# Issuing a decoder layer's input-row DMA transposes from SyncE instead of ScalarE, with its filler and priority tables refitted

## The chip, the cores and the metric

The kernel runs on one core of a Trainium2 chip. The metric is the device time of one execution in microseconds. Three runs of the kernel before gave 1943.07, 1945.29 and 1947.21 us (median 1945.29). A separate execution under the hardware profiler took 1942.91 us, of which 1941.2 us lie between its first and its last instruction (the span).

## The reference

One layer of a decoder over 2048 rows of 1024 float32 numbers:

```python
h = rms_norm(x, attn_norm_g)
z = h @ w_in                                   # 1024 x 2304
q, k, v, gate_b, gate_c, xc = split(z)         # q: 8 heads of 64; k, v: 2 heads of 64; gates and xc: 512 each
q, k = rms_norm(q, q_norm_g), rms_norm(k, k_norm_g)
y_attn = sliding_window_attention(q, k, v, sinks)        # window 128, blocks of 128 rows
y_conv = gate_b * conv3(gate_c * xc, conv_w)             # causal, over rows
y = concat(rms_norm(y_attn, attn_out_g), rms_norm(y_conv, conv_out_g))
x = x + y @ w_out
x = x + square(relu(rms_norm(x, mlp_norm_g) @ w_up)) @ w_down     # 1024 x 4096 and back
```

## The kernel before, in words

**Numbers.** Products are made of float32 numbers split into a high and a low part (`fp32r` tiles in pairs): the high part is a copy on ScalarE, the low part a subtraction on VectorE, and each product is three matmuls (`mm3`, lines 272 to 276: high by high, high by low, low by high).

**Stages.** The rows go through the mixers (attention and convolution) in four chunks of 512 rows (`mixers`, called for c = 0 to 3, each chunk four tiles of 128 rows, t = 0 to 3). This part takes the first 640 us or so. The MLP follows over all rows, in a seven-product scheme for 2 x 2 blocks (`u` in line 1485, `d` in line 1602), and takes the rest.

**Work inside a chunk.** A chunk has a chain of small steps for the attention of each block of 128 rows (`qk_norm`, `qk_transpose`, `softmax`, `values`) and a supply of long matmul groups that depend on little: the convolution's products pc, px and pb (`conv_pair`), the output projection's convolution half (`out_projection(c, 1, ..)`, tiles `pout`), and the projection of the next chunk's q, k and v (`project_qkv`, tiles `pz`). The generator `besides` hands these groups out in small pieces, and `fill(n)` puts n such pieces between two steps of the attention chain. How many go where is the table `FILL` (line 88): per chunk a pair, then four numbers groups of five, one per block. `PRIO` (line 86) holds priority offsets per chunk for fourteen kinds of steps (`ahead(i)`). A scheduler turns the program with these priorities into one in-order queue for each engine and for each engine's DMA issues; an engine does not pass a waiting instruction.

**The next chunk's rows.** While chunk c is computed, `prepare` (lines 380 to 447) makes the transposed and split input rows `h_a` of chunk c + 1, in four steps for each tile t:

- `fetch(t)` loads the tile's rows (`xt_a`, line 388; SyncE's queue).
- `halves(t)` takes the row norms (line 283 on ScalarE; GpSimd's lines 180 and 181 make the reciprocal root), scales (line 290, VectorE), takes the float32 numbers apart into their two 16-bit planes with two copies on ScalarE (line 403, `half_a`), and issues a DMA transpose of the planes back over `xt_a`: one transfer of 512 KB for t < 2 (line 407), two of 256 KB for t = 2 and 3 (line 410). That is 6 transposes a chunk and 18 in all (chunks 1 to 3 are prepared this way).
- `whole(t)` puts the planes together again with four copies on VectorE (line 417), which wait for the transposes.
- `split(t)` makes the high and low parts `h_a` (line 424 on ScalarE, line 425 on VectorE).

`EARLIER` (line 70) says after which pieces of the second convolution pair the first five steps of `prepare` are handed out; the rest are handed out three pieces apart in the output projection. For t < 2 the planes lie in buffers that the residual rows `x` of the chunk use afterwards (line 1027), so the load of those rows for t = 2 and 3 can start only when `split(0)` and `split(1)` are done.

**The convolution's norm factor.** `PC` (line 69) says after which piece of the output projection the sums for that factor are made (`pc`, line 1040); VectorE (line 1050 or 1053) and GpSimd (lines 180, 181 and, in chunk 0, 1055) turn them into `rc`, which VectorE's line 991 needs to add a `pout` result to the residual rows `x`. Line 991 also frees the PSUM bank: there are three for the `pout`, `pz` and convolution groups.

**Queues of transfers.** SyncE's queue issues, in program order as scheduled, nearly all loads and stores: stores of split weights (line 218) in chunk 0, raw weight loads (line 226: `raw_wc`, `raw_wx`, `raw_wb`, `raw_wo`), reloads of split weights in later chunks (line 235), the rows. ScalarE's and GpSimd's queues issue a few others. Each of SyncE's and ScalarE's transfers takes one of eight completion semaphores in turn, and waits until the transfer that had it has landed.

Of the kernel before, what the change touches and what calls it, by code (L numbers as in the profile page):

```python
# [11 lines left out]
U16 = mybir.dt.uint16  # L12
# [53 lines left out]
EARLY = 4  # L66
DOWN_BUFS = {"u": 2, "x1": 7}
UP_BUFS = {"w": 17, "u2": 3, "f11": 2, "u4": 2, "f12": 2, "s1": 1, "s2": 1, "s4": 1, "st": 5}
PC = (2, 1)
EARLIER = (16, 18, 23, 35, 38)  # L70

CHP = CH + 32
STEPS = 3
# [9 lines left out]

PRIO = ((60, 0, 160, -130, 30, 0, 20, -10, 0, 0, 0, 300, 0, 10), (160, -60, -120, -60, 40, 0, 20, 40, 0, -150, 0, 0, 0, -120), (80, 0, 10, 0, 40, 0, 200, -40, 0, -60, 320, 120, 0, 0), (230, 20, 180, 240, 0, 0, 40, 40, 0, 0, 0, 30, 0, 0), (160, 80, 0, 10, 0, 0, 20, -20, -20, 0, 0, 120, 0, 0))

FILL = (((14, 15), (9, 9, 11, 8, 1), (9, 6, 8, 8, 2), (10, 11, 5, 8, 4), (11, 10, 9, 6, 0)), ((25, 15), (9, 16, 11, 8, 1), (9, 10, 11, 3, 2), (13, 12, 15, 6, 5), (9, 13, 11, 5, 2)), ((20, 17), (9, 16, 11, 10, 1), (9, 5, 11, 7, 2), (16, 7, 15, 2, 6), (9, 15, 10, 5, 1)), ((27, 6), (9, 9, 5, 6, 3), (7, 7, 7, 9, 5), (4, 11, 9, 7, 8), (11, 3, 9, 3, 3)))

# [1 line left out]
def hymba_layer(  # L93
# [19 lines left out]
    nc = tc.nc  # L113
# [33 lines left out]
    def row(tag, name, bufs, dt=F32):  # L147

        return pool.tile([P, D], dt, tag=tag, name=name, bufs=bufs)
# [35 lines left out]
    def ahead(i):  # L185

        offset = PRIO[stage[0]][i]
        return tc.high_priority(offset=offset) if offset else nullcontext()
# [77 lines left out]
    @contextmanager  # L266
    def behind():

        with tc.issue_after(gates["act"]), tc.issue_after(gates["dve"]):
            yield  # L270
# [7 lines left out]
    def norm_stats(xt, name, rs=None, junk=None):  # L278
        if junk is None:
            junk = pool.tile([P, CHP], F32, tag="s2", name=f"junk_{name}", bufs=4)  # L280
        junk = junk.bitcast(BF16)[:, :D]
        ss = small.tile([P, 1], F32, tag="ss", name=f"ss_{name}", bufs=2)
        nc.scalar.activation(junk, xt, AF.Square, scale=D**-0.5, accum_out=ss)
        if rs is None:
            rs = small.tile([P, 1], F32, tag="rs", name=f"rs_{name}", bufs=2)
        rsqrt(rs, ss)
        return rs

    def scaled(xt, rs, gb):
        nc.vector.scalar_tensor_tensor(xt, xt, rs, gb, op0=ALU.mult, op1=ALU.mult)  # L290
# [88 lines left out]
    def parts(pool_, tag, name):  # L379
        return [pool_.tile([P, KD, CH], F32R, tag=f"{tag}{s}", name=f"{tag}{s}_{name}", bufs=1) for s in range(2)]  # L380

    def prepare(src, r0, gb, dst, name):

        xs, places, turned_ = {}, {}, {}

        def fetch(t):
            xs[t] = row("xt", f"xt_{name}_{t}", 2)
            nc.sync.dma_start(xs[t], src[r0 + t * P : r0 + (t + 1) * P, :])

        def halves(t):  # L390
            if t < 2:
                place = row("x1", f"half_{name}_{t}", NT)
                places[t] = [place[:, i * BW : (i + 1) * BW] for i in range(2)]
            else:
                places[t] = [
                    pool.tile([P, CHP], F32, tag="s2", name=f"half_{name}_{t}_{i}", bufs=4)[:, :BW] for i in range(2)
                ]
            xt = xs[t]
            with ahead(8), behind():
                scaled(xt, norm_stats(xt, f"{name}_{t}", junk=places[t][0]), gb)  # L400
                pairs = xt.bitcast(U16).rearrange("p (c i) -> p i c", i=2)
                for i, plane in enumerate(places[t]):
                    nc.scalar.copy(plane.bitcast(U16), pairs[:, i])
                turned_[t] = xt.bitcast(U16).rearrange("p (i k t) -> p i k t", i=2, k=KD)
                if t < 2:
                    out = xt.bitcast(U16).rearrange("p (k t) -> p k t", t=P)
                    nc.scalar.dma_start_transpose(out, place.bitcast(U16))
                else:
                    for i, plane in enumerate(places[t]):
                        nc.scalar.dma_start_transpose(turned_[t][:, i], plane.bitcast(U16))  # L410

        def whole(t):
            with ahead(9), behind():
                for n, raw in enumerate(places[t]):
                    pairs = raw.bitcast(U16).rearrange("p (k t i) -> p i k t", k=KH, i=2)
                    for i in range(2):
                        nc.vector.tensor_copy(pairs[:, i], turned_[t][:, i, n * KH : (n + 1) * KH])

        def split(t):
            with ahead(9), behind():  # L420
                for n, raw in enumerate(places[t]):
                    raw = raw.rearrange("p (k t) -> p k t", k=KH)
                    dh, dl = (d[:, n * KH : (n + 1) * KH, t * P : (t + 1) * P] for d in dst)
                    nc.scalar.copy(dh, raw)
                    nc.vector.tensor_tensor(dl, raw, dh.bitcast(F32), op=ALU.subtract)

        fetch(0)
        fetch(1)
        yield
        for t in range(2):  # L430
            halves(t)
            yield
        for t in range(2):
            whole(t)
            fetch(t + 2)
            yield
        dst += parts(pool, "h", name)
        for t in range(NT):
            split(t)
            if t < 2:  # L440
                halves(t + 2)
            if 0 < t < NT - 1:
                whole(t + 1)
            yield
# [218 lines left out]
    with tc.tile_pool(name="mix_small", bufs=1) as mix_small, tc.tile_pool(name="mix", bufs=1) as mix:  # L663
# [342 lines left out]
        def besides(c, before, h, yt, rc, x1, h_next, z_next):  # L1006
# [6 lines left out]
            else:  # L1013
                steps = range(PC[0] + 1)
            for j in range(2):
                for n, _ in enumerate(conv_pair(c, h, j, yt, ssc)):
                    if blocks and n % X_EVERY == 0:
                        next(blocks, None)
                    if j and not blocks and n in EARLIER:
                        next(steps)  # L1020
# [9 lines left out]
            for i, _ in enumerate(steps):  # L1030
                if c + 1 == NCHUNK:
                    yield
                for j in range(STEPS):
                    next(out, None)
                    yield
                    if (i, j) == PC:
                        factors.update((c, 1, t) for t in range(NT))
# [24 lines left out]
        def mixers(c, before, h, z):  # L1062


            last = c + 1 == NCHUNK
            n_fill = FILL[c]
            stage[0] = c
# [574 lines left out]
```

## Time and profile before

| | us |
|---|---|
| median of three runs | 1945.29 |
| profiled execution | 1942.91 |
| its span | 1941.2 |
| TensorE busy in the span | 1911.1 |
| VectorE, ScalarE, GpSimd busy | 1221.1, 850.4, 281.7 |
| DMA transposes: issues | 18, from ScalarE's queue |

A row of the timeline gives the start, the duration, the engine, the line of the kernel, the operation, output and inputs, how many such instructions are merged, and in brackets how long the engine was idle before the first of them and what ended that. ACTq and SPq are the issuing of DMAs by ScalarE and SyncE, which the busy times leave out. In a row of the windows each engine has its busy time and its number of instructions, and behind them stand the granted TensorE clock as a share of full speed, the mean busy share of the 16 DMA engines and the bytes moved per second. A matmul's recorded duration is longer than its spacing from the next one, since matmuls overlap; a 512-column one starts 0.23 us after the one before when nothing holds it.

### The profile page before, as it was taken

The page shows a single profiled execution, that of the slowest core. Times are in us where ns is not written, and L with a number is a line of the kernel's source. Part 1 is how long each engine was busy: PE and PEld are TensorE (multiplying, and loading weights), DVE is VectorE, ACT ScalarE, POOL GpSimd, SP SyncE. Part 2 cuts the span into 40 slices and gives each one's busy share as a digit, 9 for nine tenths or more (in the row PEclk, how much of TensorE's full clock was granted, in tenths as well). Part 3 has the DMA queues.
Part 4 walks back from the last instruction along what each step waited for, and adds up shares of the span by engine and source line. Part 5 has one row for each costly group of instructions (what it writes and reads, how often), then busy time and mean ns, then how long its engine had stood idle before and what let it go on. Part 6 is the DMA issues. An engine that isn't in the chain of part 4 may idle for free.

```text
span 1941.2 us, 24490 instructions
## 1 busy us (share of the span) xinstructions
PE 1911.1 (98%) x8834; PEld 1588.8 (82%) x8834; DVE 1221.1 (63%) x1905; ACT 850.4 (44%) x1581; POOL 281.7 (15%) x477
## 2 busy tenths in 40 slices
PE   9979999999899999999999999999999999999999
PEld 8868887888788888888888888888888888888887
DVE  4876567546648759998878766666544334447441
ACT  6554455435535337445565555554422332232220
POOL 2121312302131111222201111111000000100000
PEclk9989999999999999999999999999999999999999
DMA  9996858356567868878676544437964447766641
GB/s 299 317 255 198 275 221 267 133 217 225 176 230 264 292 210 271 249 210 241 202 231 225 184 147 152 159 124 295 375 224 138 148 161 237 260 228 207 204 152 55
DMA packets 257946, 420.11 MB, mean 216 GB/s; under 512 B 76824, under 2 KB 161568, under 8 KB 245024
## 3 DMA queue, kind: packets, MB, share of 16 engines
q1 hardware_dynamic: 203840, 336.59, 51.8%
q0 software_dynamic: 15424, 51.40, 6.9%
q10 hardware_dynamic: 38560, 30.55, 5.3%
q8 instruction: 70, 1.15, 0.2%
q14 instruction: 52, 0.43, 0.1%
HBM read 286.35 MB, written 125.83 MB: 212 GB/s over the span
## 4 chain that ended last, share of the span: by engine, by line
PE 80%; DVE 1%; ACT 1%; POOL 1%; ACTq 1%; issue 0%; DMA 0%; DVEq 0%
PE u L1485 31%; PE d L1602 31%; PE pout L274 2%; PE pout L275 2%; PE pout L276 2%; PE pz L274 1%; PE pz L276 1%; PE pz L275 1%; PE px_c L274 1%; PE px_c L276 1%; PE px_c L275 1%; PE pb_c L274 1%; PE pb_c L276 1%; PE po_b L838 1%; PE pb_c L275 1%; PE pc_c L275 1%
## 5 line engine op out<-in xcount | busy, mean ns | idle before, releaser
L1485 PE MATMUL u<-op_x,wop 128*128 128x512 f32 x2688 | 609.8, 389 | 0.0
L1602 PE MATMUL d<-op_w,op_f 128*128 128x512 f32 x2691 | 609.5, 389 | 0.0
L1485 PEld LDWEIGHTS u<-op_x,wop 128*128 128x128 f32 x2688 | 504.5, 188 | 105.1 <-issue 0.6
L1602 PEld LDWEIGHTS d<-op_w,op_f 128*128 128x128 f32 x2691 | 504.8, 188 | 104.7
L460 DVE TENSOR_TENSOR op_f<-op_f 128x1024 fp32r<-128x1024 f32 x112 | 136.8, 1224 | 235.8 <-ACT op_f L459 235.3
L459 ACT CAST op_f<-op_f 128x1024 fp32r<-128x1024 f32 x112 | 117.5, 1051 | 352.2 <-DMA op_f<-fop 342.2
L478 ACT CAST wop<-wu 128x512 fp32r<-128x512 f32 x156 | 96.2, 619 | 90.6 <-PE u L1485 88.2
L479 DVE TENSOR_TENSOR wop<-wu,wop 128x512 fp32r<-128x512 f32 x156 | 110.8, 712 | 32.3 <-DMA wu<-in_w_up_dram 20.1
L1221 POOL DMA_DIRECT2D fop<-s x96 | 52.1, 542 | 441.1 <-DVE s L1224 434.5
L1227 DVE TENSOR_TENSOR u<-u,u 128x512 f32<-128x512 f32 x128 | 87.7, 685 | 21.2 <-PE u L1485 20.9
L460 DVE TENSOR_TENSOR op_w<-raw,op_w 128x1024 fp32r<-128x1024 f32 x56 | 68.3, 1221 | 27.0 <-ACT op_w L459 26.8
L459 ACT CAST op_w<-raw 128x1024 fp32r<-128x1024 f32 x56 | 58.8, 1052 | 46.3 <-PE d L1602 24.2
L1233 ACT ACTIVATE u<-u 128x512 f32<-128x512 f32 x64 | 40.5, 632 | 58.9 <-DVE u L1227 56.8
L799 POOL TENSOR_SCALAR_AFFINE_SELECT pp_b<-pp_b 128x512 fp32r<-128x512 f32 x60 | 42.5, 720 | 149.3 <-ACT pp_b L792 115.3
L767 ACT ACTIVATE sc_b<-sc_b,ngm_b 128x128 f32<-128x128 f32 x128 | 49.7, 390 | 28.3 <-DVE ngm_b L764 26.4
L274 PE MATMUL pout<-w_wo,yt_c 128*128 128x512 f32 x128 | 53.2, 418 | 8.4 <-DVE x L991 8.0
L750 PE MATMUL psc_b<-kw,qt_b 128*128 128x256 f32 (+1 forms) x256 | 51.6, 292 | 6.0 <-DVE qt_b L729 5.1
L1434 POOL DMA_DIRECT2D wds<-raw x16 | 8.5, 533 | 330.5 <-DVE raw L1432 330.5
L275 PE MATMUL pout<-w_wo,yt_c 128*128 128x512 f32 x128 | 52.3, 409 | 1.6 <-DVE w_wo L247 1.6
L479 DVE TENSOR_TENSOR wop<-wu_s,wop 128x512 fp32r<-128x512 f32 x64 | 45.9, 718 | 12.3 <-ACT wop L478 12.2
L761 DVE COPY_PREDICATED sc_b<-later,psc_b 128x128 f32<-128x128 int32 x120 | 29.0, 295 | 38.8 <-ACT sc_b L758 38.6
L478 ACT CAST wop<-wu_s 128x512 fp32r<-128x512 f32 x64 | 39.4, 620 | 30.1 <-PE u L1485 24.5
(241 smaller groups left out, 3159.2 us busy)
## 6 DMA issues: line engine op xcount, KB each, us to landing
op_f<-fop SPq DMA_DIRECT2D x112, 512.0 KB, 4.3
raw<-in_w_down_dram SPq DMA_DIRECT2D x72, 512.0 KB, 4.4
wu<-in_w_up_dram SPq DMA_DIRECT2D x128, 256.0 KB, 3.7
w_wo<-wo SPq DMA_DIRECT2D x24, 1024.0 KB, 6.8
fop<-s POOLq DMA_DIRECT2D x96, 256.0 KB, 2.8
fop<-u ACTq DMA_DIRECT2D x64, 256.0 KB, 2.6
op_x<-xop SPq DMA_DIRECT2D x28, 512.0 KB, 6.0
w_q<-q SPq DMA_DIRECT2D x12, 1024.0 KB, 6.9
```

Source lines behind the costliest of these rows:

```text
L274: nc.tensor.matmul(ps, st(0), mv(0), start=first, stop=False)
L275: nc.tensor.matmul(ps, st(0), mv(1), start=False, stop=False)
L276: last_sum[0] = nc.tensor.matmul(ps, st(1), mv(0), start=False, stop=last).ins
L459: nc.scalar.copy(op[:, 0], raw)
L460: nc.vector.tensor_tensor(op[:, 1], raw, op[:, 0].bitcast(F32), op=ALU.subtract)
L478: splits.append(nc.scalar.copy(hi, blk).ins)
L479: lows.append(nc.vector.tensor_tensor(lo, blk, hi.bitcast(F32), op=ALU.subtract).ins)
L750: nc.tensor.matmul(ps[:, j].rearrange("p s k -> p (s k)")[:, :nk], qt[:, pr, j, :], kw[:, r, kv, :, :].rearrange("p s k -> p (s k)")[:, :n ...
L1221: eng.dma_start(fop_dram[tb][ORDER_DOWN.index(i)][n // 2][:, n % 2], b)
L1227: return nc.vector.tensor_tensor(dst, ps, b, op=ALU.add).ins
L1485: nc.tensor.matmul(pt, wops[i][:, a, k, :], xops[tb, p][k // 2][:, b, k % 2, :], start=p not in GOES_ON and k + j == 0, stop=k + j == NB + ...
L1602: nc.tensor.matmul(ps[tb][j][:, cs], fs[tb][:, a, k, j * P : (j + 1) * P], w[:, b, k, cs], start=first and p not in GOES_ON and k + n == 0 ...
```

## The change

The DMA transposes of `prepare` are issued by SyncE. They take their place in SyncE's queue among the loads and stores. `PC` and `EARLIER` have other numbers, and so have the tables `FILL` and `PRIO`, of which one line each is shown in part; 13 of the 88 numbers of `FILL` and 14 of the 70 of `PRIO` differ. No operation is added or removed: the instructions are the same, in another order on each engine.

```diff
-PC = (2, 1)
-EARLIER = (16, 18, 23, 35, 38)
+PC = (1, 2)
+EARLIER = (14, 19, 23, 35, 37)
...
-FILL = (((14, 15), (9, 9, 11, 8, 1), (9, 6, 8, 8, 2), (10, 11, 5, 8, 4), (11, 10, 9, 6, 0)),
+FILL = (((18, 15), (9, 9, 11, 8, 1), (9, 6, 4, 8, 2), (10, 11, 5, 8, 4), (11, 10, 9, 2, 0)),
...
                 if t < 2:
                     out = xt.bitcast(U16).rearrange("p (k t) -> p k t", t=P)
-                    nc.scalar.dma_start_transpose(out, place.bitcast(U16))
+                    nc.sync.dma_start_transpose(out, place.bitcast(U16))
                 else:
                     for i, plane in enumerate(places[t]):
-                        nc.scalar.dma_start_transpose(turned_[t][:, i], plane.bitcast(U16))
+                        nc.sync.dma_start_transpose(turned_[t][:, i], plane.bitcast(U16))
```

The scheduler's queues differ as follows at three places. In the names, the number at the end tells one buffer from another. The first is ScalarE in chunk 0, where the planes of tile 1 (`half_a_1`) are made. Before:

```order
L403 COPY half_a_1_1217<-xt_a_1_1157 128x1024
L846 COPY o_b_1246<-po_b_0_1237 64x512
L403 COPY half_a_1_1217<-xt_a_1_1157 128x1024
L728 CAST qt_b_1257<-ptq_b_1258 64x4x128
L730 CAST kw<-ptk_b_1263 64x128
L731 CAST kw<-ptk_b_1263 64x128
L846 COPY o_b_1246<-po_b_1_1243 64x512
L407 DMA_TRANSPOSE xt_a_1_1157<-half_a_1_1217 128x16x128
L728 CAST qt_b_1257<-ptq_b_1258 64x4x128
```

And now, at the same place of ScalarE:

```order
L403 COPY half_a_1_1217<-xt_a_1_1132 128x1024 x2
L246 ACTIVATE w_wo_0_1481<-raw_wo_1479,g_y 128x512 x2
L728 CAST qt_b_1276<-ptq_b_1277 64x4x128
L730 CAST kw<-ptk_b_1282 64x128
L731 CAST kw<-ptk_b_1282 64x128
L846 COPY o_b_1265<-po_b_0_1249 64x512
L846 COPY o_b_1265<-po_b_1_1262 64x512
L728 CAST qt_b_1276<-ptq_b_1277 64x4x128
```

The transpose is gone from between the two halves of the query tile `qt_b`, and two splits of the output weight `w_wo`, which need the load `raw_wo`, now stand ahead of the first half; before, they stood behind the second.

The second place is SyncE's queue around the same two transposes of chunk 0 (`wx`, `wb` and `wo` on the left are stores of split weights, `raw_wo` are loads). Before:

```order
L218 DMA wx_0_1147<-w_wx_0_1137 128x2048
L218 DMA wx_1_1148<-w_wx_1_1138 128x2048
L1027 DMA x_0_0_1453<-in_x_dram 128x1024
L1027 DMA x_0_1_1455<-in_x_dram 128x1024
L226 DMA raw_wo_1479<-in_w_out_dram 128x4x512
L218 DMA wb_0_1308<-w_wb_0_1298 128x2048
L218 DMA wb_1_1309<-w_wb_1_1299 128x2048
L226 DMA raw_wo_1665<-in_w_out_dram 128x4x512
```

And now:

```order
L1027 DMA x_0_0_1453<-in_x_dram 128x1024
L407 DMA_TRANSPOSE xt_a_0_1130<-half_a_0_1168 128x16x128
L1027 DMA x_0_1_1455<-in_x_dram 128x1024
L226 DMA raw_wo_1479<-in_w_out_dram 128x4x512
L218 DMA wx_0_1151<-w_wx_0_1141 128x2048
L218 DMA wx_1_1152<-w_wx_1_1142 128x2048
L218 DMA wb_0_1308<-w_wb_0_1298 128x2048
L407 DMA_TRANSPOSE xt_a_1_1132<-half_a_1_1217 128x16x128
L218 DMA wb_1_1309<-w_wb_1_1299 128x2048
L226 DMA raw_wo_1665<-in_w_out_dram 128x4x512
```

The two stores of `wx` have moved behind the first `raw_wo` load, the first transpose stands ahead of that load, and the second transpose stands between the two stores of `wb`, ahead of the second `raw_wo` load.

The third place is SyncE's queue at the transposes of tiles 2 and 3 in chunk 0, beside the loads of the query weights `w_q` for chunk 1. Before:

```order
L235 DMA w_q_0_1796<-q_918 128x2048
L235 DMA w_q_1_1793<-q_510 128x2048
L235 DMA w_q_1_1797<-q_918 128x2048
L218 DMA wo_1_1678<-w_wo_1_1668 128x2048
L235 DMA w_qkv_0_1800<-qkv_0_506 128x2048
```

And now:

```order
L235 DMA w_q_0_1796<-q_918 128x2048
L235 DMA w_q_1_1797<-q_918 128x2048
L235 DMA w_q_1_1793<-q_510 128x2048
L410 DMA_TRANSPOSE xt_a_2_1329<-half_a_2_0_1467 128x8x128
L410 DMA_TRANSPOSE xt_a_2_1329<-half_a_2_1_1468 128x8x128
L218 DMA wo_0_1677<-w_wo_0_1667 128x2048
L410 DMA_TRANSPOSE xt_a_3_1341<-half_a_3_0_1509 128x8x128
L410 DMA_TRANSPOSE xt_a_3_1341<-half_a_3_1_1510 128x8x128
```

The transposes of tile 2 stand directly behind three loads of 1 MB.

More of the change, by code (lines that the diff above doesn't have):

```diff
@@ L82 @@
 SOON = 330
-PRIO = ((60, 0, 160, -130, 30, 0, 20, -10, 0, 0, 0, 300, 0, 10), (160, -60, -120, -60, 40, 0, 20, 40, 0, -150, 0, 0, 0, -120), (80, 0, 10, 0, 40, 0, 200, -40, 0, -60, 320, 120, 0, 0), (230, 20, 180, 240, 0, 0, 40, 40, 0, 0, 0, 30, 0, 0), (160, 80, 0, 10, 0, 0, 20, -20, -20, 0, 0, 120, 0, 0))
-FILL = (((14, 15), (9, 9, 11, 8, 1), (9, 6, 8, 8, 2), (10, 11, 5, 8, 4), (11, 10, 9, 6, 0)), ((25, 15), (9, 16, 11, 8, 1), (9, 10, 11, 3, 2), (13, 12, 15, 6, 5), (9, 13, 11, 5, 2)), ((20, 17), (9, 16, 11, 10, 1), (9, 5, 11, 7, 2), (16, 7, 15, 2, 6), (9, 15, 10, 5, 1)), ((27, 6), (9, 9, 5, 6, 3), (7, 7, 7, 9, 5), (4, 11, 9, 7, 8), (11, 3, 9, 3, 3)))
+PRIO = ((60, 0, 160, -70, 30, 0, 20, -10, -130, 0, 0, 300, 0, 10), (160, -60, -120, -60, 40, 110, 20, 40, 0, -150, 0, 0, 0, -120), (140, 0, 10, -10, 40, 0, 200, -40, 0, -90, 260, 150, 0, -10), (230, 20, 180, 360, 0, 0, 0, 40, 0, 0, -10, 30, 30, -60), (160, 80, 0, 10, 0, 0, 20, -20, -20, 0, 0, 120, 0, 0))
+FILL = (((18, 15), (9, 9, 11, 8, 1), (9, 6, 4, 8, 2), (10, 11, 5, 8, 4), (11, 10, 9, 2, 0)), ((24, 16), (9, 16, 10, 8, 1), (9, 10, 11, 3, 2), (13, 12, 15, 6, 5), (9, 13, 11, 5, 3)), ((20, 17), (9, 16, 11, 10, 1), (8, 5, 11, 7, 2), (16, 11, 15, 0, 6), (9, 13, 10, 5, 1)), ((28, 6), (9, 7, 5, 6, 3), (7, 7, 7, 9, 5), (4, 11, 9, 7, 8), (11, 3, 9, 3, 3)))
 @with_exitstack
```

## The prediction

> **What bounds the kernel now.** The table of windows comes first, because it separates the stages. Its columns are the length, the busy times of PE, PEld, DVE, ACT and POOL, the granted TensorE clock, the DMA share and GB/s.
>
> ```profile
> span 1941.2 us, 24490 instructions
> ...
> 0.00:60.00 60.00, 58.34 (x318) 50.61 (x319) 32.38 (x56) 33.83 (x66) 16.51 (x41) 1.00 0.93 317
> 60.00:200.00 140.00, 128.73 (x637) 107.62 (x636) 101.82 (x211) 76.83 (x197) 22.86 (x38) 0.95 0.81 244
> 200.00:340.00 140.00, 136.20 (x662) 113.56 (x661) 93.67 (x197) 68.02 (x173) 33.39 (x53) 1.00 0.74 256
> 340.00:480.00 140.00, 136.48 (x684) 115.00 (x683) 77.74 (x165) 59.95 (x168) 32.90 (x53) 0.99 0.50 185
> 480.00:640.00 160.00, 154.05 (x788) 127.86 (x787) 105.34 (x216) 79.20 (x202) 35.87 (x58) 0.98 0.66 232
> 640.00:1300.00 660.00, 659.91 (x2944) 546.86 (x2943) 510.41 (x766) 341.51 (x582) 114.21 (x186) 1.00 0.63 206
> ```
>
> From 640 us on, in the MLP, TensorE has no gap and full clock: a change to the mixers can win nothing there. Between 60 and 640 us it idles 580 − (128.73 + 136.20 + 136.48 + 154.05) = 24.5 us, and the clock is below 1 in places. That is all there is to win. So I read TensorE's timeline of the mixers next, for the gaps and what ended them:
>
> ```profile
> 115.12 3.36 PE L750 MATMUL psc_b<-kw,qt_b 128*128 128x256 f32 x14 [5.12 <-DVE qt_b L729]
> 127.68 0.50 PE L275 MATMUL pout<-w_wo,yt_c 128*128 128x512 f32 x1 [1.63 <-DVE w_wo L247]
> 129.57 0.71 PE L274 MATMUL pout<-w_wo,yt_c 128*128 128x512 f32 x1 [0.44 <-ACT yt_c L925]
> 146.25 0.50 PE L274 MATMUL pout<-w_wo,yt_c 128*128 128x512 f32 x1 [3.58 <-DVE x L991]
> 333.29 0.50 PE L274 MATMUL pz<-w_q,h_a 128*128 128x512 f32 x1 [1.35 <-DVE x L991]
> 377.29 0.49 PE L838 MATMUL po_b<-pp_b,vd 128*128 128x512 f32 x1 [2.94 <-POOL pp_b L799]
> 505.89 0.80 PE L274 MATMUL pout<-w_wo,yt_c 128*128 128x512 f32 x1 [4.43 <-DVE x L991]
> ```
>
> These seven gaps are 19.5 of the 24.5 us. A gap also costs clock afterwards, which finer windows show:
>
> ```profile
> 115.00:120.00 5.00, 4.88 (x20) 4.55 (x21) 4.92 (x15) 4.48 (x10) 0.00 (x0) 0.55 1.14 155
> 129.00:133.00 4.00, 3.56 (x13) 2.85 (x13) 4.00 (x8) 4.00 (x8) 0.00 (x0) 0.59 0.38 84
> 146.50:151.00 4.50, 4.50 (x14) 3.52 (x14) 2.69 (x5) 1.99 (x2) 0.00 (x0) 0.62 0.31 129
> 506.00:512.00 6.00, 6.00 (x14) 4.68 (x15) 4.90 (x11) 3.37 (x10) 0.00 (x0) 0.50 0.35 67
> ```
>
> Work at clock s for b us loses (1 − s)·b: 2.2, 1.5, 1.7 and 3.0 us.
>
> Last, ScalarE's timeline at the two longest gaps, and the line of the 512 KB transposes, with issue times in ns (min/median/max) and time to landing:
>
> ```profile
> 103.93 9.79 ACTq L407 DMA_TRANSPOSE xt_a<-half_a  x1
> 113.76 0.58 ACT L728 CAST qt_b<-ptq_b 64x512 fp32r<-64x512 f32 x1 [8.34 <-issue]
> ...
> 495.82 8.62 ACTq L410 DMA_TRANSPOSE xt_a<-half_a  x2
> 504.48 0.65 ACT L758 COPY sc_b<-psc_b 128x256 f32<-128x256 f32 x2 [8.43 <-issue]
> ```
>
> ```profile
> L407 ACTq DMA_TRANSPOSE xt_a<-half_a x6: 1595/2137/9789, 90.9 to 463.5; - x6
> DMA to landing us min/median/max: 3.7/5.7/18.2
> ```
>
> ScalarE's next computation waits until its DMA issue is over. Twice that took over 8 us, and TensorE ran dry behind it: first for the second half of qt_b, then for L991, which VectorE had queued behind work on ScalarE's score copy L758.
>
> **The change part by part.**
>
> *The transposes leave ScalarE.* At 103.93 the issue stands between two halves of qt_b (first place in the order); that is gone. The 5.12 us gap and its 2.2 us of clock go: 7.3 us. At 495.82 the 4.43 us and 3.0 us go: 7.4 us. The other 15 issues stalled ScalarE where TensorE had other work; I count nothing for them.
>
> By the Trainium skill (DMA: Bandwidth & Descriptors, "Issuing engines are not separate DMA queues"), starting DMAs from another engine saves only the sequencer's issue time, usually small beside the transfer. Here the row of 9.79 us is over half of the longest landing, 18.2 us, so I do not take "small" over; by the rule, the sum would be near nothing.
>
> *The gap at 126 us* (1.63 + 0.44 + 1.5 of clock, 3.6 us) has another root. VectorE stood at L417, waiting for the same transpose to land:
>
> ```profile
> 123.65 0.46 DVE L417 COPY half_a<-xt_a 128x512 uint16<-128x512 uint16 x1 [2.72 <-DMA xt_a<-half_a]
> ```
>
> A transpose on SyncE's queue still has to land. Ends: 0 and 3.6; I take half, 1.8, since the first 2 MB of stores (wx) now stand behind raw_wo and the transpose of tile 0 (second place).
>
> *PC and GpSimd's order.* The gap at 146.25 waits for rc:
>
> ```profile
> 145.44 2.07 DVE L991 SCALAR_TENSOR_TENSOR x<-pout,rc,x 128x512 f32<-128x512 f32 x3 [2.87 <-POOL rc L1055]
> 142.75 0.56 POOL L181 TENSOR_TENSOR ra<-ms_b,mhalf 128x1 f32<-128x1 f32 x1
> 143.39 0.22 POOL L180 TENSOR_SCALAR ss_a<-ss_a 128x1 f32<-128x1 f32 x1
> 144.71 0.54 POOL L181 TENSOR_TENSOR rs_a<-ss_a,mhalf 128x1 f32<-128x1 f32 x1
> 145.21 0.20 POOL L1055 TENSOR_TENSOR rc<-rc,rs 128x4 f32<-128x4 f32 x1
> ```
>
> Three small operations for other things (1.3 us) stood inside the chain from ms_c to rc; with the new PC the pc sums come some four matmuls (0.9 us) earlier, and in GpSimd's new order the three are outside the chain. Ends 0 and 3.58 + 1.7 = 5.3; I take 2.4, the 1.6 us by which the idle shrinks to about 2 and half of the clock loss.
>
> Gross: 7.3 + 7.4 + 1.8 + 2.4 = 18.9 us.
>
> *What it adds.* SyncE now waits for the planes, then issues, by the L407 line, for 1.6 to 9.8 us, with loads queued behind it. In chunks 1 and 2 most of these are reloads of weights (L235), which wait for TensorE to release their buffers anyhow:
>
> ```profile
> SPq L235 <- PE pout L276: 81.2, 10, 18.4
> ```
>
> For them I take nothing. In chunk 0 the second raw_wo load is behind a transpose (second place):
>
> ```profile
> 109.11 0.38 SPq L226 DMA_DIRECT2D raw_wo<-in_w_out_dram  x1
> DMA to landing us min/median/max: 13.6/14.2/14.8
> ```
>
> It used to leave at 109.11, after a wait for the first transpose's semaphore. Behind an issue from about 104 on it leaves between 105 and 114 and lands between 119 and 128; if it is late, ScalarE stands at the split of w_wo with pp_b behind it, and TensorE waits for that. I take nothing, ends 0 and 4. Directly ahead of tile 2's transposes in chunk 0 now stand three 1 MB loads (third place). By 244 GB/s of the 60:200 row, 1 MB is 4.3 us; their pz is some 90 matmuls, 20 us, away in TensorE's order, so I take 1.5 us, ends 0 and 6. Elsewhere at most one such load stands ahead, but chunk 1 has no slack: the gap at 333.29 is this chain, a transpose landing, then L417, then L991:
>
> ```profile
> 325.18 6.79 DMA xt_a<-half_a
> 332.49 0.76 DVE x L991
> ```
>
> A later landing is TensorE's loss here: 2 us, ends 0 and 5.9 (4.3 of transfer, 1.6 of clock). The load of the residual rows of tile 2 (L1027) can now start only close to pc, and L991 waits for it: its landing takes 3.3 to 11.5 us, median 7.2, against some 30 matmuls (7 us) and the 2 us of idle until TensorE needs the bank:
>
> ```profile
> DMA to landing us min/median/max: 3.3/7.2/11.5
> ```
>
> I take 1.5, ends 0 and 5. The other new fillers and priorities move the order everywhere in the mixers. Gaps like that at 377.29 (GpSimd) may come or go; no row prices that, so 0, ends −3 and +3. New costs: 1.5 + 2 + 1.5 = 5.0.
>
> Net: 18.9 − 5.0 = 13.9. The profiled execution took 1942.9 us (1.7 outside the span), so 1929.0; the median lies 2.4 higher at 1945.3, which makes **1931.4**.
>
> **The rivals.**
>
> *The bytes set the pace (no change).* Both long issues fall where DMA is full:
>
> ```profile
> 501.00:506.00 5.00, 0.57 (x4) 0.15 (x2) 1.11 (x3) 1.52 (x4) 0.00 (x0) 0.92 1.02 341
> 85.00:165.00 80.00, 68.73 (x306) 55.58 (x305) 59.09 (x112) 44.69 (x108) 12.09 (x20) 0.91 0.93 272
> ```
>
> If a share of 1 is the ceiling, the stretch from 85 to 165 can lose 7% of 80, 5.6 us, and the one around 500 nothing. That less 5.0 of new costs is 0.6: 1944.7. Against it: the first 60 us moved 317 GB/s at 0.93, so share is not bytes; the 21.8 MB of that stretch (80 us at 272 GB/s) take 69 us at that rate. What the rule on issue time in the part above comes to is the same: nothing won. Chance 0.14.
>
> *Late landings ahead of the evacuations (slower).* Tiles 2 and 3 in three chunks make six places where L417 stands ahead of some L991 in VectorE's queue. If each landing comes one 1 MB load later, a place costs 4.3 + 1.6 = 5.9 us as in chunk 1. Three places cost 17.7 and leave the time about as it was; four, 23.6, turn the sign: −18.9 + 23.6 = +4.7, so 1950; six give +16.5, 1962. The price needs a transpose to queue behind what SyncE issued before it. Against it: L417 waited for landings only for 9.7 us in all, five times:
>
> ```profile
> DVE half_a L417 <- DMA xt_a<-half_a: 9.7, 5, 3.1
> ```
>
> The Trainium skill (same page, "Queues, rings and completion order") says that each DMA engine takes a ring's descriptors in order, and that SyncE and ScalarE have a ring each on it; by that, this rival's premise holds, and no run yet shows it. Chance 0.17, at 1950.
>
> *ScalarE waits there for raw_wo instead (smaller gain).* Two splits of w_wo now stand ahead of qt_b. If raw_wo still lands 13.6 us after the 95.19 of its row, at 108.8, ScalarE, which comes there at about 104, loses 5 of the 8.34 us again:
>
> ```profile
> 95.19 1.43 SPq L226 DMA_DIRECT2D raw_wo<-in_w_out_dram  x1
> ```
>
> Then 5.3 of the 7.3 us are not won: 1936.7. Against it: two stores (2 MB) that were ahead of that load are behind it now. Chance 0.12.
>
> **How the numbers follow.** The forecast has 0.57, the rivals 0.14, 0.17 and 0.12. The forecast's own range goes from 1921.7 (18.9 raised to its upper end, 23.6, and no new cost) to 1938 (new costs of 11.6 instead of 5.0). I give 1921 to 1946: it takes in the forecast, the smaller gain and no change, and leaves out the slower case. A change of 0.2% (3.9 us) is about what a measurement here can tell. Faster, below 1941.4: 0.57 + 0.12 + a fifth of the 0.14, 0.72; same: 0.11; slower: 0.17.
>
> **What would show it.** Right: no ACTq transposes; no idle of ScalarE by "issue" over 3 us; no gap over 3 us before psc at about 110 and before pout at about 500; clock 1.0 behind them; PE's idle from 60 to 640 us near 14 us; transposes in SPq with issues as long as before. Wrong: SPq rows of many us with TensorE, VectorE or ScalarE waiting for loads behind them; L417 waiting for landings well over 9.7 us in all, with L991 and gaps behind it; a gap before psc with ScalarE at L246 for raw_wo.

## The result, and the profile after

The changed kernel took 1921.91 us (median of four runs, 1920.14 to 1927.52) against 1945.15 us before in the same comparison: ratio 0.9885, interval 0.9862 to 0.9909. It is faster, by 23 us where 13.9 were forecast, and lies near the lower end of the range.

The windows of the changed kernel, with the columns of the prediction's first fence:

```profile
span 1918.4 us, 24487 instructions
...
60.00:200.00 140.00, 137.19 (x707) 115.03 (x706) 116.36 (x240) 87.32 (x218) 29.17 (x47) 1.00 0.85 269
200.00:340.00 140.00, 139.39 (x673) 115.37 (x672) 87.47 (x187) 67.72 (x181) 31.08 (x51) 1.00 0.66 233
340.00:480.00 140.00, 137.60 (x687) 115.44 (x686) 83.17 (x175) 64.57 (x167) 32.17 (x54) 0.99 0.61 219
480.00:640.00 160.00, 157.33 (x821) 131.14 (x820) 107.96 (x230) 72.21 (x190) 33.58 (x57) 1.00 0.71 246
640.00:1300.00 660.00, 659.98 (x2924) 546.38 (x2924) 507.89 (x748) 349.15 (x585) 115.03 (x185) 1.00 0.62 202
```

TensorE's idle time between 60 and 640 us is 580 − 571.5 = 8.5 us, from 24.5: 16.0 us of the gain. Its busy time in the whole span fell from 1911.1 to 1904.0 us, though the matmuls are the same; I read these 7.1 us as time that it had spent at a slow clock (the losses quoted ahead of the prediction's sum were 8.4). Together they are 23.1, and the span is 22.8 us shorter. All of it is in the mixers; the MLP is as it was.

Only two gaps of TensorE over 1 us are left there, the second and third of these rows of its timeline:

```profile
119.36 0.50 PE L275 MATMUL pout<-w_wo,yt_c 128*128 128x512 f32 x1 [0.31 <-DVE w_wo L247]
133.12 0.50 PE L274 MATMUL pout<-w_wo,yt_c 128*128 128x512 f32 x1 [1.42 <-DVE x L991]
...
356.46 0.50 PE L838 MATMUL po_b<-pp_b,vd 128*128 128x512 f32 x1 [1.98 <-POOL pp_b L799]
```

The two long ones (5.12 us before psc, 4.43 us before pout at 506 us) are gone, the one for w_wo (1.63 us) is down to 0.31, the one for rc went from 3.58 to 1.42 us, the one for GpSimd from 2.94 to 1.98. The clock behind the rc gap is 1.00 now (0.62 before); behind the GpSimd gap it is still low, 0.72 from 356 to 362 us.

```profile
133.00:138.00 5.00, 4.88 (x23) 4.11 (x24) 4.86 (x11) 1.02 (x3) 0.24 (x1) 1.00 0.68 220
```

The transposes themselves, on SyncE's queue (issue ns min/median/max, first and last start, then time to landing; 512 KB ones first, then the 256 KB ones):

```profile
L407 SPq DMA_TRANSPOSE xt_a<-half_a x6: 1602/1634/4826, 89.3 to 446.1; - x6
DMA to landing us min/median/max: 3.7/3.7/6.6
L410 SPq DMA_TRANSPOSE xt_a<-half_a x12: 1237/1318/5051, 144.1 to 481.1; - x12
  DVE half_a L417: 2.8, 3
DMA to landing us min/median/max: 3.3/4.5/9.0
```

The long issues are shorter (512 KB: at most 4.8 us, from 9.8; 256 KB: at most 5.1, from 7.2), and the transposes land earlier (512 KB: median 3.7 us, from 5.7, and at most 6.6, from 18.2; 256 KB: median 4.5, from 4.8, and at most 9.0, from 11.6). L417's waits for landings fell from 9.7 us to 2.8 us; all of these lie between 477 and 489 us.

### The profile page after: what moved, and what is told of

The parts are those of the page before. It is cut to its first block, busy times and chain, and to the rows that moved or that the text cites. A ratio compares the mean times of both kernels' runs of the same rounds, so it can differ in the third digit from the quotient of the medians.

```text
span 1918.4 us, 24487 instructions
## 1 busy us (share of the span) xinstructions
PE 1904.0 (99%) x8834; PEld 1582.6 (82%) x8834; DVE 1218.4 (64%) x1905; ACT 850.9 (44%) x1581; POOL 280.8 (15%) x477
## 4 chain that ended last, share of the span: by engine, by line
PE 92%; DVE 2%; DMA 2%; ACT 2%; POOL 1%; issue 0%; SPq 0%; DVEq 0%; POOLq 0%; ACTq 0%
PE d L1602 32%; PE u L1485 32%; PE pout L274 2%; PE pout L275 2%; PE pout L276 2%; PE pc_c L276 2%; PE pc_c L274 2%; PE pc_c L275 2%; PE pz L275 1%; PE pz L274 1%; PE pz L276 1%; PE px_c L274 1%; PE px_c L275 1%; PE px_c L276 1%; PE psc_b L750 1%; PE pb_c L274 1%
## 5 line engine op out<-in xcount | busy, mean ns | idle before, releaser
L799 POOL TENSOR_SCALAR_AFFINE_SELECT pp_b<-pp_b 128x512 fp32r<-128x512 f32 x60 | 43.3, 733 | 139.0 <-ACT pp_b L792 101.5
L767 ACT ACTIVATE sc_b<-sc_b,ngm_b 128x128 f32<-128x128 f32 x128 | 49.6, 389 | 20.0 <-DVE ngm_b L764 19.9
L274 PE MATMUL pout<-w_wo,yt_c 128*128 128x512 f32 x128 | 50.8, 398 | 2.0 <-DVE x L991 2.0
L274 PE MATMUL pb_c<-h_a,w_wb 128*128 128x512 f32 x128 | 51.0, 398 | 0.0
L276 PE MATMUL pb_c<-h_a,w_wb 128*128 128x512 f32 x128 | 50.6, 395 | 0.0
```

What stands on the lines that cost most here:

```text
L274: nc.tensor.matmul(ps, st(0), mv(0), start=first, stop=False)
L276: last_sum[0] = nc.tensor.matmul(ps, st(1), mv(0), start=False, stop=last).ins
```

## The experiments

All kernels but the two with extra copies do exactly the work of the kernel before, in another order or from another queue. Each ratio is to the kernel before, timed on the same chip; its median was 1944.05 us beside the first four kernels, 1947.73 beside the second four and 1943.63 beside the last four, so the ratios are what to compare.

### The two halves of the change

**move_only**: the transposes on SyncE in the kernel before, and nothing else.

```diff
-                    nc.scalar.dma_start_transpose(out, place.bitcast(U16))
+                    nc.sync.dma_start_transpose(out, place.bitcast(U16))
...
-                        nc.scalar.dma_start_transpose(turned_[t][:, i], plane.bitcast(U16))
+                        nc.sync.dma_start_transpose(turned_[t][:, i], plane.bitcast(U16))
```

> The kernel before with all 18 transposes on SyncE and the old PC, EARLIER, FILL and PRIO. Theory 1 (ScalarE's issue time was the cost): the gaps before psc at about 110 us and before pout at about 501 us and the slow clock behind them go, 7.3 + 7.4 us, and 1 to 3 us of the one at 126; the gap for rc near 146 stays at about 3.5 us. About 1929 us, TensorE idle from 60 to 640 us 12 to 15 us. Theory 2 (the refitted tables bring it; the move alone only changes which queue waits): within 5 us of the kernel before, 1940 to 1950, with new gaps behind late loads or landings.

1933.11 us, ratio 0.9944 (0.9925 to 0.9963): 11 us. The gap before psc at 110 us is gone, and the one near 500 us is down to 0.97 us. The rc gap stays, and smaller ones stand behind it (TensorE's timeline):

```profile
135.82 0.57 PE L274 MATMUL pout<-w_wo,yt_c 128*128 128x512 f32 x1 [3.35 <-DVE x L991]
...
149.00 0.71 PE L750 MATMUL psc_b<-kw,qt_b 128*128 128x256 f32 x4 [1.06 <-DVE o_b L847]
151.50 0.79 PE L275 MATMUL pout<-w_wo,yt_c 128*128 128x512 f32 x1 [1.78 <-DVE w_wo L247]
```

**tables_only**: the new tables, PC and EARLIER, with the transposes still issued by ScalarE (the changed kernel with the diff above turned round).

> The changed kernel with the transposes back on ScalarE. Theory 1: ScalarE's issues over 4 us come back where DMA is full (about 104 and 480 us), ScalarE idles by issue, and TensorE has at least one gap over 3 us behind it; what the tables save by themselves is the gap for rc, 2 to 5 us: about 1940. Theory 2: most of the gain stays, 1920 to 1928.

1956.89 us, ratio 1.0064 (1.004 to 1.0087): slower than before, which neither theory had. ScalarE's timeline, then TensorE's:

```profile
89.57 11.29 ACTq L407 DMA_TRANSPOSE xt_a<-half_a  x1
100.91 0.40 ACT L767 ACTIVATE sc_b<-sc_b,ngm_b 128x128 f32<-128x128 f32 x1 [11.36 <-issue]
```

```profile
121.35 0.77 PE L750 MATMUL psc_b<-kw,qt_b 128*128 128x256 f32 x2 [4.69 <-DVE o_b L847]
```

An issue of 11.29 us now holds back the softmax's exponentials (L767), and the attention chain behind them is late. Near 510 us two issues together hold ScalarE for 10.2 us, and at 311 us VectorE waits 9.2 us at L417 for a landing, with 4.47 us of TensorE's idle time behind it. The two halves do not add up: the tables cost 12 us while ScalarE issues and gain about 11 once SyncE does. My reading is that they fit an engine whose work is not interrupted.

### One place at a time

**move_c0** and **move_c2**: in the kernel before, only the six transposes issued in chunk 0 (or in chunk 2) are on SyncE.

```diff
-                    nc.scalar.dma_start_transpose(out, place.bitcast(U16))
+                    (nc.sync if name == "a1" else nc.scalar).dma_start_transpose(out, place.bitcast(U16))
```

(The same at the second call; "a3" for chunk 2.)

> The kernel before, with only the six transposes of chunk 0 (those of chunk 1's rows) issued by SyncE; tables, PC and EARLIER as before. Theory (ScalarE's issue time is the cause, place by place): the 5.12 us gap before psc at 110 us and its slow clock go, 7.3 us, and the gap at 126 us perhaps too; the move alone in all chunks left new small gaps of some 3 us between 145 and 152 us, which stand here as well; so 3 to 7 us faster than before, about 1939, with the 4.43 us gap before pout near 500 us still there. Rival (the gain needs all chunks, since moved transfers only shift the load elsewhere): within 2 us of before.

> The kernel before, with only the six transposes of chunk 2 issued by SyncE. Theory: the 4.43 us gap before pout near 500 us and its slow clock go, 6 to 7.4 us, about 1937.5; the gaps of chunk 0 (5.12 us at 110 us, 3.58 us at 146 us) stay. The two single moves then add up to about the 11 us of the move in all chunks. Rival (the bytes set the pace there, DMA share 1.02): the gap stays under another name, waiting for a landing instead, and the time is within 2 us of before.

move_c0: 1941.07 us, ratio 0.9976 (0.9959 to 0.9993), 4.7 us. move_c2: 1935.48 us, ratio 0.9945 (0.9924 to 0.9966), 10.7 us. Each long gap goes with its own transposes, all but 0.96 us near 500 us, and the other stays. TensorE in move_c0, then in move_c2:

```profile
138.86 0.80 PE L274 MATMUL pout<-w_wo,yt_c 128*128 128x512 f32 x1 [2.20 <-DVE x L991]
...
504.93 0.80 PE L274 MATMUL pout<-w_wo,yt_c 128*128 128x512 f32 x1 [4.11 <-DVE x L991]
```

```profile
115.28 3.36 PE L750 MATMUL psc_b<-kw,qt_b 128*128 128x256 f32 x14 [5.23 <-DVE qt_b L729]
...
494.25 0.50 PE L274 MATMUL pout<-w_wo,yt_c 128*128 128x512 f32 x1 [0.96 <-DVE x L991]
```

The single moves would come to 0.9921 together, the move in all chunks gave 0.9944 (0.9925 to 0.9963); within the intervals they add up. Chunk 1's six transposes were not moved by themselves; the sum leaves nothing for them that can be seen. Chunk 0 gives back a part of its 7.3 us in small gaps further on, as in move_only.

### What in the tables does it

**pc_only**: the kernel before with the new PC. **after_pc21**: the changed kernel with the old one.

```diff
-PC = (2, 1)
+PC = (1, 2)
```

> The kernel before with PC = (1, 2) alone. If PC by itself cuts the gap for rc: the gap near 146 falls to about 1.5 us, 2 to 4 us gained, 1941 to 1943; the two gaps behind ScalarE's issues stay. If not, 1945, with the gap still at 3.5 us.

> The changed kernel with PC back at (2, 1). If the new PC is what cut the gap for rc in chunk 0 from 3.58 to 1.42 us: the gap is back at 3 to 4 us with about 1.7 us of slow clock, 2 to 4 us more than the changed kernel, 1924 to 1926. If the rest of the order did that: 1922, the gap below 2 us.

pc_only: 1948.53 us, ratio 1.0024 (1.0004 to 1.0045). after_pc21: 1923.48 us, ratio 0.9892 (0.9869 to 0.9916), beside 0.9885 for the whole change. The rc gap follows the other tables and not PC. (In the profile of pc_only an issue of 12.67 us stands before psc, and TensorE idles 8.87 us behind it.) The rc gap in pc_only and in after_pc21:

```profile
152.19 0.79 PE L274 MATMUL pout<-w_wo,yt_c 128*128 128x512 f32 x1 [3.34 <-DVE x L991]
```

```profile
134.95 0.50 PE L274 MATMUL pout<-w_wo,yt_c 128*128 128x512 f32 x1 [1.42 <-DVE x L991]
```

**move_newprio** and **move_newfill**: the move with the whole new PRIO, or with the whole new FILL, and the rest as before.

> The kernel before, with all transposes on SyncE and the new priorities (PRIO); FILL, PC and EARLIER as before. The move alone gave 1933.1 and everything together 1921.9. Theory (the rest of the gain is in the order of the small steps, the chain to rc among them): the rc gap near 135 us falls from 3.35 to about 1.4 us and the time to 1924 to 1929. Rival (the tables work only together): 1931 or more, with gaps of over 2 us in other places.

> The kernel before, with all transposes on SyncE and the new fillers (FILL); PRIO, PC and EARLIER as before. Theory (priorities hold most of the rest of the gain): the rc gap near 135 us stays at over 3 us and the time at 1930 to 1934. Rival (the fillers hold it): 1923 to 1928, with the GpSimd gap near 372 us shorter. Second rival (neither works alone): slower than the move alone, 1934 to 1940.

move_newprio: 1926.23 us, ratio 0.9906 (0.988 to 0.9933). move_newfill: 1935.49 us, ratio 0.9948 (0.9925 to 0.9971), no different from the move alone. The expected gap for rc of over 3 us is not there, though: it is 1.59 us, and a longer one stands before it. In move_newfill, TensorE, VectorE and GpSimd:

```profile
140.96 0.80 PE L750 MATMUL psc_b<-kw,qt_b 128*128 128x256 f32 x2 [6.85 <-DVE qt_b L729]
```

```profile
138.90 1.28 DVE L290 SCALAR_TENSOR_TENSOR xt_a<-xt_a,rs_a,g_attn 128x1024 f32<-128x1024 f32 x1 [1.22 <-POOL rs_a L181]
140.22 0.69 DVE L729 TENSOR_TENSOR qt_b<-ptq_b,qt_b 64x512 fp32r<-64x512 f32 x1
```

```profile
143.82 0.24 POOL L180 TENSOR_SCALAR ms_c<-ms_c 128x4 f32<-128x4 f32 x1 [1.22 <-DVE ms_c L1053]
...
145.57 0.20 POOL L1055 TENSOR_TENSOR rc<-rc,rs 128x4 f32<-128x4 f32 x1
```

Here rc is ready 1.95 us after ms_c starts, and none of the three small operations stands between them. But the second half of qt_b stands behind the scaling of the next chunk's rows (L290), and TensorE waits for it. **after_oldfill**, the changed kernel with the old FILL:

> The changed kernel with the old FILL. The new fillers alone brought nothing to the move (ratio 0.9948 against 0.9944), the new priorities brought most of the rest (0.9906). Theory (the priorities hold the rest, the fillers a remainder): 0.2% or so above the changed kernel, ratio to before about 0.990 to 0.991, with gaps of 1 to 2 us at 167, 191 and 591 us as in the run with new priorities alone. Rival (fillers are worth nothing): the changed kernel's ratio, 0.9885, within 0.1%.

1927.68 us, ratio 0.992 (0.9903 to 0.9936), so the new fillers are worth perhaps 0.3% beside the new priorities, PC and EARLIER; the intervals (0.9862 to 0.9909 with them) just overlap, and the size stays open. EARLIER was not tried alone.

**move_prio8**: the move with one number of the 70 of PRIO changed, the priority in chunk 0 of `halves` (norm, scaling, plane copies and transposes of the next chunk's rows).

```diff
-PRIO = ((60, 0, 160, -130, 30, 0, 20, -10, 0, 0, 0, 300, 0, 10),
+PRIO = ((60, 0, 160, -130, 30, 0, 20, -10, -130, 0, 0, 300, 0, 10),
```

> The kernel before, with all transposes on SyncE and one priority changed: the norm, scaling and plane copies of the next chunk's rows (halves) get -130 instead of 0 in chunk 0. Theory (this number took GpSimd's ss_a and rs_a out of the chain to rc): the rc gap near 135 us falls from 3.35 to about 1.5 us, and the time from the move's ratio of 0.9944 to 0.991 to 0.993. Rival (the chain is set elsewhere, or other new priorities did it): the rc gap stays over 3 us and the ratio at 0.994 or above.

1925.35 us, ratio 0.9904 (0.9888 to 0.9921): about 8 us more than the move alone, from one number, and within the interval of the whole change. GpSimd's timeline around rc, in move_only and in move_prio8:

```profile
132.01 0.24 POOL L180 TENSOR_SCALAR ms_c<-ms_c 128x4 f32<-128x4 f32 x1
132.32 0.56 POOL L181 TENSOR_TENSOR ra<-ms_b,mhalf 128x1 f32<-128x1 f32 x1
132.96 0.22 POOL L180 TENSOR_SCALAR ss_a<-ss_a 128x1 f32<-128x1 f32 x1
133.26 1.05 POOL L181 TENSOR_TENSOR rc<-ms_c,mhalf 128x4 f32<-128x4 f32 x1
134.28 0.54 POOL L181 TENSOR_TENSOR rs_a<-ss_a,mhalf 128x1 f32<-128x1 f32 x1
134.78 0.20 POOL L1055 TENSOR_TENSOR rc<-rc,rs 128x4 f32<-128x4 f32 x1
```

```profile
133.70 0.24 POOL L180 TENSOR_SCALAR ms_c<-ms_c 128x4 f32<-128x4 f32 x1
134.02 1.05 POOL L181 TENSOR_TENSOR rc<-ms_c,mhalf 128x4 f32<-128x4 f32 x1
135.15 0.20 POOL L1055 TENSOR_TENSOR rc<-rc,rs 128x4 f32<-128x4 f32 x1
```

The chain from ms_c to rc is 1.65 us long instead of 2.97, as expected. But rc itself is ready at 135.35 and not at 134.98: it is not earlier, since ms_c starts 1.69 us later. What else changed is the order on VectorE. The second half of the next block's qt_b stood behind the scaling of tile 3 (L290) and now stands ahead of it. VectorE's timeline in move_only, then in move_prio8:

```profile
137.00 1.27 DVE L290 SCALAR_TENSOR_TENSOR xt_a<-xt_a,rs_a,g_attn 128x1024 f32<-128x1024 f32 x1
138.31 0.69 DVE L729 TENSOR_TENSOR qt_b<-ptq_b,qt_b 64x512 fp32r<-64x512 f32 x1
```

```profile
133.65 0.69 DVE L729 TENSOR_TENSOR qt_b<-ptq_b,qt_b 64x512 fp32r<-64x512 f32 x1
...
138.50 1.28 DVE L290 SCALAR_TENSOR_TENSOR xt_a<-xt_a,rs_a,g_attn 128x1024 f32<-128x1024 f32 x1
```

With qt_b complete at 134.3 instead of 139.0 us, TensorE has its psc as work before it needs the bank that L991 frees. Its timeline in move_prio8 has no idle time from the second of these rows to 160 us:

```profile
134.39 1.22 PE L750 MATMUL psc_b<-kw,qt_b 128*128 128x256 f32 x4 [0.98 <-DVE qt_b L729]
136.19 0.80 PE L274 MATMUL pout<-w_wo,yt_c 128*128 128x512 f32 x1 [0.57 <-DVE x L991]
```

TensorE's busy time from 60 to 640 us is 568.5 us, against 563.2 with the move alone: 5.3 of the 7.1 us by which the span is shorter (1923.9 against 1931.0). The chain on GpSimd and the steps on VectorE were freed by the same number. Two runs above speak for the second: in move_newfill the chain is short but qt_b stands behind L290, and nothing is gained; in after_oldfill two of the small operations are inside the chain (2.33 us from ms_c to rc) but qt_b is ahead of L290, and the ratio is 0.992. Other steps move in both runs too, so this is not a test of the one order alone.

### Does a transpose wait behind its own queue's transfers?

**after_copy_sp** and **after_copy_act**: the changed kernel with two additional stores of 512 KB, the planes to a scratch area in DRAM, written in the program directly ahead of each of the six 512 KB transposes. The transposes stay on SyncE; the stores are issued by SyncE or by ScalarE. (Behind the insertion the lines count two more, so L407 is L409.)

```diff
+                    for i in range(2):
+                        nc.sync.dma_start(dram.tile([P, 2 * D], U16, name=f"copy_{name}_{t}_{i}"), place.bitcast(U16))
                     nc.sync.dma_start_transpose(out, place.bitcast(U16))
```

> The changed kernel with 1 MB of copies (two stores of 512 KB of the planes to a scratch area in DRAM) issued by SyncE directly ahead of each of the six 512 KB transposes. Theory (a transpose queues behind what its own queue issued before): its landing grows by the megabyte, about 4 us at 246 GB/s, from a median of 3.7 to 7 us or more, and L417 waits. Rival (all queues share the engines, only bytes count): it grows as much as when ScalarE issues the copies. Second rival (it lands at once): 3.7 us still.

> The changed kernel with the same 1 MB of copies ahead of each of the six 512 KB transposes, but issued by ScalarE, the transposes by SyncE as in the changed kernel. Theory (own queue counts): landing of the transposes stays near 4 us or grows by half of what it grows with SyncE's copies. Rival (bytes count): the same growth as with SyncE's copies. In both cases ScalarE loses what its six pairs of issues take; near 0.4 us each that is 5 us, a part of it on TensorE's path.

The line of the transposes in after_copy_sp, then in after_copy_act:

```profile
L409 SPq DMA_TRANSPOSE xt_a<-half_a x6: 3289/4223/7132, 90.2 to 450.8; - x6
DMA to landing us min/median/max: 5.4/6.8/9.2
```

```profile
L409 SPq DMA_TRANSPOSE xt_a<-half_a x6: 4731/4873/7774, 89.3 to 456.9; - x6
DMA to landing us min/median/max: 8.0/9.2/12.5
```

Counted from the start of the transpose's issue, a megabyte in the same queue delays the landing by 3.1 us (6.8 against 3.7), a megabyte in the other queue by 5.5 us. But the two do not leave alike. SyncE's two copies start 0.9 to 1.3 us ahead of the transpose; ScalarE's leave at the same moment as it, since neither queue waits for the other. SyncE and ScalarE in after_copy_act:

```profile
89.29 6.16 SPq L409 DMA_TRANSPOSE xt_a<-half_a  x1
```

```profile
89.29 0.84 ACTq L408 DMA_DIRECT2D copy_a<-half_a  x2
```

Counted from the first issue of copy or transpose, the six landings have medians of about 7.7 us (SyncE's copies) and 9.2 us (ScalarE's), worked out from the starts and landings of each; in chunk 0 the two are about level (9.7 and 10.5 us against 9.2 and 11.1). So a place behind one's own queue costs no more than bytes that another queue put in flight: the first theory, by which the own queue counts more, is not borne out. Whether the other queue's bytes cost more stays open. Most of the growth behind SyncE's copies and more than half of it beside ScalarE's is in the issue itself: the median goes from 1.63 us to 4.22 and 4.87 us.

The times: after_copy_sp 1923.62 us, ratio 0.9897 (0.9883 to 0.9912), not to be told from the changed kernel, though it moves 6 MB more in the same 600 us; after_copy_act 1932.07 us, ratio 0.9938 (0.9923 to 0.9953). Bytes do not set the pace of this kernel. The 8 us between the two are one megabyte six times on the other queue, with its later landings and twelve issues on ScalarE: the waits of L417 (L419 here) for the 512 KB landings come to 9.7 us there, and to 0.3 us with SyncE's copies. Which of the two costs more was not parted.

## Why the prediction was right or wrong

**What bounds the kernel: right.** The gain lies within the idle time and the slow clock that were named, and nothing beyond 640 us changed.

**The transposes leave ScalarE (7.3 and 7.4): right.** Both gaps went with the issue, each by itself when only its transposes moved (4.7 us, interval 1.4 to 8.0, and 10.7 us, interval 6.6 to 14.8). For chunk 1 no run speaks against the forecast's zero. The Trainium skill (DMA: Bandwidth & Descriptors, "Issuing engines are not separate DMA queues") says two things that are tested here. That transfers of several engines interleave on the same hardware agrees with the 9.2 us landing beside ScalarE's copies. That only issue time is saved, usually a small one, agrees in part: the gaps that went stood behind issues, but these were not small, and moving them was worth 11 us; the issues also became shorter and the landings earlier.

**The gap at 126 us (1.8): mis-sized.** Half of it was expected to stay behind a landing; 0.31 us stays, with no loss of clock (1.00 from 118 to 125 us), so the term is 3.6 less 0.3. The move alone may not bring all of that: with it a gap of 1.78 us for w_wo stands at 151.50 us.

**PC and GpSimd's order (2.4): the size too small, one cause wrong.** The gap fell by 2.2 us and its 1.7 us of slow clock went as well, 3.9 together. "With the new PC the pc sums come some four matmuls earlier" does no work: the gap is 1.42 us with either PC. The other half, three small operations inside the chain to rc, is what one priority takes out in move_prio8, but that number also puts qt_b ahead of the row preparation on VectorE, and rc did not come earlier for it. In move_newfill the chain is free of the three and nothing is won.

**What it adds (5.0): failed.** This is the larger part of the miss, and each piece of it is nil. The three w_q loads did not hold tile 2's transposes up: the loads had left SyncE by 140.8 us, and the transposes left at 144.15 us, when their planes were ready (L403 ends at 144.12). In chunk 0 L417 never waited for a landing. The second raw_wo load left at 109.43 us, about as before (109.11). In chunk 1 the chain of landing, L417 and L991, 1.35 us of idle at 333 us, has 0.25 us at its worst (307.68 us). The rows of L1027 land in 4.5 us at the median where they took 7.2, and L991 never waits for them. The premise was that a transpose on SyncE queues behind SyncE's bulk transfers, is issued as slowly as before and lands later. SyncE's timeline in the changed kernel gives a reason why it does not:

```profile
89.28 4.51 SPq L407 DMA_TRANSPOSE xt_a<-half_a  x1
...
94.95 0.97 SPq L218 DMA_DIRECT2D wx<-w_wx  x2
```

The two stores of wx (2 MB) start only when the transpose has been issued. SyncE can't put bulk in flight while it waits for planes and issues them, whereas with ScalarE issuing, it did so right ahead and beside: in tables_only the two stores of wx leave just ahead of the transpose that took 11.29 us to issue, at 89.57 us:

```profile
85.59 2.33 SPq L218 DMA_DIRECT2D wx<-w_wx  x2
```

By the copies, a megabyte of another queue adds 3.2 us to an issue of 1.6; two would make 8.0, an estimate to set beside 9.79 and 11.29. That this is the whole reason was not tried by itself.

**The other fillers and priorities (0, −3 to +3): too narrow.** The tables as a whole turn from +12 us to −11 us with the engine that issues. Within the forecast's sum that is hidden, since it took the changed order as it stood; but as "refitted numbers bring nothing" it would have been wrong.

By terms: 18.9 as forecast, +1.5 at 126 us, +1.5 at rc, +1.0 at the GpSimd gap, no new costs: 22.9, and the span is 22.8 shorter. That the two meet so closely is partly luck. These terms hold 14.4 us of idle time and 8.4 of slow clock where 16.0 and 7.1 were measured, and gaps of 1.35 us at 333 us and 1.20 us at 213 us, which no term of the gain held, went too. The range held only just, by 0.9 us: its lower end had been worked out from both doubtful terms in full and no new cost, and that is nearly what came. Two of the signs did not hold: TensorE's idle time is 8.5 us where about 14 were expected, and the issues are not as long as before (at most 4.8 us, from 9.8).

**The rivals.** Bytes: refuted, 6 MB more cost no time that can be told. Late landings: refuted, they are earlier, and the Trainium skill's rule (same page, "Queues, rings and completion order"), by which each engine has a ring of its own taken in order, does not by itself decide the landing: the megabyte in the own ring delays it no more than the one in the other. ScalarE waiting for raw_wo: absent where the rival put it. At the two splits ahead of qt_b ScalarE waited 0.30 us, for TensorE. It waited 0.61 us for raw_wo at 118 us, for the second load; TensorE's only gap nearby, 0.31 us at 119.36, ended on VectorE's L247:

```profile
104.21 1.34 ACT L246 ACTIVATE w_wo<-raw_wo,g_y 128x512 fp32r<-128x512 f32 x2 [0.30 <-PE px_c L275]
...
118.13 1.34 ACT L246 ACTIVATE w_wo<-raw_wo,g_y 128x512 fp32r<-128x512 f32 x2 [0.61 <-DMA raw_wo<-in_w_out_dram]
```

## What to carry to other kernels

Look at how long a DMA's issue holds the queue of the engine that issues it, above all for transposes (1.6 us and more for 512 KB here, where a store of 512 KB took 0.3 to 0.5), and at which computations stand behind it. Where that engine feeds the busiest one, move the issue to an engine that computes nothing, and refit the order afterwards: here the refitted order was worth as much again with the move, and cost 12 us without it. Before charging later landings to the move, ask what the new issuer can no longer put in flight meanwhile. And when an idle gap ends on a chain of small operations, look as well at which preparatory work has priority over the steps that feed the waiting engine: here one priority was worth 8 us.

## What the runs showed of the hardware

- The issue of a 512 KB transpose took 1.6 us in chunks 1 and 2 of the changed kernel (mean DMA share 0.27 to 0.30 during the issue), 4.5 and 4.8 us in its chunk 0 (share 1.14 and 1.01), and up to 12.7 us from ScalarE (pc_only); with 1 MB just ahead of it or beside it, never under 3.3 us. In these runs the length of an issue follows the traffic.
- The slow clock came without a long gap, too. In move_prio8 the clock fell to half just before 132 us and stayed there to 142 us (the row below shows the first 8 us). The gaps of TensorE before that are 0.44, 0.54 and 0.25 us, and from 129.1 us on it had begun only two 512-column matmuls and some of one column (the gaps of 0.98 and 0.57 us came after the fall). In the changed kernel one gap of 1.42 us cost none. The Trainium skill (TensorE: Matmul & The Clock Gate, "Part 1: The HAM clock gate") has the gate watch activity in free-running windows of some 3.4 us; a sum over such a window fits the two cases better than the length of a single gap, but two cases are no test of it.

```profile
132.00:140.00 8.00, 6.45 (x20) 5.30 (x21) 6.02 (x11) 4.28 (x9) 3.75 (x7) 0.50 1.10 254
```
